# Sparse attention of a two-layer trunk: float32 operands replaced by two float16 parts in three passes

## The chip, the cores and the metric

One core of one Trainium2 chip runs the whole program. The metric is the time of one execution on the device in microseconds (us). An engine takes its instructions in an order that is fixed when the kernel is built.

## What is computed

A trunk of two layers over 512 tokens of width 1024. Each layer first normalises, projects and runs two branches (an RWKV-7 recurrence and a sparse attention), merges them with gates and projects again; then comes attention into 256 memory tokens, then a SwiGLU (layer 0) or eight experts (layer 1). The change lies in the sparse attention, cut here to its core (top_k is 128, eight heads of 64, one shared key and value head):

```python
logits = einsum('bqhd,bsd->bqhs', qib, k_idx32) * (IDX_DIM ** -0.5)
score = einsum('bqhs,bqh->bqs', relu(logits), wb) * (IDX_HEADS ** -0.5)
score = where(admissible[None], score, NEG_INF)
_, sel = lax.top_k(score, top_k)
ks, vs = gather(k, sel), gather(v, sel)
s = einsum('bqhd,bqkd->bqhk', qb, ks) * (DSA_HEAD_DIM ** -0.5)
p = softmax(where(valid[:, :, None, :], s, NEG_INF), axis=-1)
out = einsum('bqhk,bqkd->bqhd', p, vs)
```

## The kernel before

Matmuls with weights already run as float16 pairs: a float32 operand is kept as a high part and a low part (the remainder), and three passes (high by high, low by high, high by low) go into one PSUM bank. `split_ps` (L197) makes such a pair from a PSUM bank: ScalarE writes the high part, then VectorE subtracts it from the bank and writes the low part. The sparse attention does not do so: its operands are float32.

A layer is put together from generators that are stepped by a string (`ORDER`, L1633): `r` the recurrence, `d` keys and queries of the sparse attention, `s` its selection, `a` its attention, `g` the sixteen gate projections, `b` the branch projections. A scheduler then fixes each engine's order of instructions; the string only sets who comes first when several could go. Gates, recurrence and sparse attention therefore stand interleaved in the queue of TensorE (PE).

- `keys_queries` (L396) projects keys, values and index keys, normalises and rotates them, transposes them on PE, and copies them out of PSUM: `kT` (L421, ScalarE), `ikT` (L422, VectorE), `vt` (L409, ScalarE). `queries` (L459) does so for `iqT` and `qT`, by one ScalarE copy per bank (L487). Each key is stored twice, on partitions 0 to 63 and 64 to 127, and a pair of heads shares one tile: head e of a pair lies on row half e.
- `select` (L489), for the blocks b = 1 to 3 of 128 queries with n = 128(b+1) keys: for each of eight heads one float32 matmul of 64 rows by n columns into a bank of the two-bank group `att` (L503), a relu on ScalarE (L505), a weighted sum on VectorE (L507, L509); then sixteen rounds of MAX8 and MATCH_REPLACE on VectorE (L513, L514), which leave a mask.
- `attend` (L517), for each block, each half jp of the heads and each row half e: two score matmuls (L529) into `att` banks; VectorE adds the mask and takes the maximum (L530); ScalarE takes the exponential and scales by the reciprocal sum (L534, L538). After a `yield`, which lets the next attend's scores come first: transposes of the probabilities into `att` banks (L546), one copy of each bank to float32 `pT` (L547, on ScalarE for the first two key tiles and on VectorE for the others), and the product with the values (L553), whose output takes 64 partitions, half e of the bank `po`. After e = 1 the bank is split into `ybh` and `ybl` and stored.

The changed functions, with their callers:

Of the kernel before, what the change touches and what calls it, by code (L numbers as in the profile page):

```python
# [54 lines left out]
class Kern:  # L55
# [315 lines left out]
    def dsa(self, l, hh, hl, ybd, cx):  # L371
# [13 lines left out]
        qT = dp.tile([P, 4, SEQ], F32, name="qT")  # L385
        masks = [dp.tile([P, (b + 1) * P], BF, name=f"mask{b}") for b in range(NT)]
        ip = pool("dsai", 1, c1)
        iqT = ip.tile([P, 4, SEQ], F32, name="iqT")
        ikT = ip.tile([P, SEQ], F32, name="ikT")
# [3 lines left out]
        def keys_queries():  # L393
            with ExitStack() as c2:
# [5 lines left out]
                for i in range(2):  # L400
# [8 lines left out]
                    nc.scalar.activation(vt[:, t2, :], p[:, :, 64:128], AF.Copy, scale=1 / SW)  # L409
# [11 lines left out]
                    nc.scalar.copy(kT[:, cs].rearrange("p (t c) -> p t c", t=2), pv[:, :, 0, :])  # L421
                    nc.vector.tensor_copy(ikT[:, cs].rearrange("p (t c) -> p t c", t=2), pv[:, :, 1, :])  # L422
# [17 lines left out]
        def attends():  # L440
            todo = []
            for b in range(NT):
                if b == 0:
                    c2 = ExitStack()
                    dw = pool("dsav", 1, c2)
                if b == 2:
                    next(todo.pop(0), None)
                    c2.close()
                    c1.close()
                    dw = pool("dsaw", 2, cx)  # L450
                for jp in range(2):
                    for e in range(2):
                        todo.append(self.attend(dw, b, jp, e, masks[b], qT, kT, vt, qs, ybd))
                        next(todo[-1])
                        if len(todo) > 1:
                            next(todo.pop(0), None)
                yield
            next(todo.pop(0), None)
            cx.close()  # L459
        return keys_queries(), selects(), attends()  # L460

    def queries(self, pp, hh, hl, c, c0, dst, tabs, qs):
# [3 lines left out]
        for cc in range(2):  # L466
            ps = self.proj_tok2([c(c0 + 256 * cc, c0 + 256 * cc + 256)], hh, hl)
            for i in range(2):
# [15 lines left out]
                for j in range(4):  # L484
                    nc.tensor.transpose(pt[:, j * P:(j + 1) * P], qr[:, j // 2, 2 * (j % 2):2 * (j % 2) + 2, :].rearrange("p a b -> p (a b)"),
                                        self.ident)
                nc.scalar.copy(dst[:, 2 * cc:2 * cc + 2, 2 * i * P:(2 * i + 2) * P].rearrange("p j (t c) -> p t j c", t=2),  # L487
                               pt.rearrange("p (t j c) -> p t j c", t=2, j=2))

    def select(self, dw, b, m, iqT, ikT, iw):  # L490
# [9 lines left out]
        for h in range(8):  # L500
            hs = slice((h % 2) * 64, (h % 2) * 64 + 64)
            pl = self.bank("att", "pl")
            nc.tensor.matmul(pl[:, :n], lhsT=iqT[hs, h // 2, bs], rhs=ikT[hs, :n], start=True, stop=True)  # L503
# [13 lines left out]
    def attend(self, dw, b, jp, e, mask, qT, kT, vt, qs, ybd):  # L517

        nc = self.nc
        n = (b + 1) * P  # L520
        bs = slice(b * P, (b + 1) * P)
        es = slice(e * 64, e * 64 + 64)
        nm = 2 * P if b < 2 else SEQ
        s2 = dw.tile([P, 2, nm], F32, name="s2", bufs=2)
        mx, nb, sm, rv = (dw.tile([P, 2], F32, name=x, bufs=2) for x in ("mx", "nb", "sme", "rv"))
        q2 = qs[:, b, 4 * jp + e:4 * jp + e + 3:2]
        for i in range(2):
            pl = self.bank("att", "psc")
            nc.tensor.matmul(pl[:, :n], lhsT=qT[es, 2 * jp + i, bs], rhs=kT[es, :n], start=True, stop=True)  # L529
            nc.vector.tensor_tensor_reduce(s2[:, i, :n], pl[:, :n], mask, 1.0, -3.0e38, OP.add, OP.max, mx[:, i:i + 1])  # L530
        nc.vector.scalar_tensor_tensor(nb, mx, -1.0, q2, OP.mult, OP.mult)
        for i in range(2):
            h = 4 * jp + 2 * i + e
            nc.scalar.activation(s2[:, i, :n], s2[:, i, :n], AF.Exp, bias=nb[:, i:i + 1], scale=qs[:, b, h:h + 1],  # L534
                                 accum_out=sm[:, i:i + 1])
        nc.vector.reciprocal(rv, sm)
        for i in range(2):
            nc.scalar.activation(s2[:, i, :n], s2[:, i, :n], AF.Copy, scale=rv[:, i:i + 1])  # L538
        yield
        pT = dw.tile([P, nm // P, 2 * P], F32, name="pT", bufs=1)  # L540
        for k2 in range(0, b + 1, 2):
            m = min(2, b + 1 - k2)
            pp = self.bank("att", "pp")
            for x in range(2 * m):
                kt = k2 + x // 2
                nc.tensor.transpose(pp[:, x * P:(x + 1) * P], s2[:, x % 2, kt * P:(kt + 1) * P], self.ident)  # L546
            (nc.scalar.copy if k2 == 0 else nc.vector.tensor_copy)(  # L547
                pT[:, k2:k2 + m, :], pp[:, 0:2 * m * P].rearrange("p (k c) -> p k c", k=m))
        if e == 0:
            self.po = self.bank("po", "po")  # L550
        po = self.po
        for kt in range(b + 1):
            nc.tensor.matmul(po[es, 0:2 * P], lhsT=vt[:, kt, :], rhs=pT[:, kt, :], start=kt == 0, stop=kt == b)  # L553
        if e == 1:
            yh = dw.tile([P, 2, P], F16, name="ybh")
            yl = dw.tile([P, 2, P], F16, name="ybl")
            self.split_ps(yh, yl, po[:, 0:2 * P].rearrange("p (j t) -> p j t", j=2))
            for d, y in zip(ybd, (yh, yl)):
                nc.sync.dma_start(d[2 * jp:2 * jp + 2, :, bs].rearrange("j p t -> p j t"), y)
# [1195 lines left out]
```

## Time and profile before

| | |
|---|---|
| median of 3 runs | 2184.46 us (2177.66 to 2187.46) |
| the profiled execution | 2181.56 us, span 2179.8 us |
| PE busy | 2038.4 us (94%) |
| VectorE (DVE) busy | 1368.0 us (63%) |
| ScalarE (ACT) busy | 987.9 us (45%) |
| GpSimd (POOL) busy | 325.7 us (15%) |
| mean granted TensorE clock | 0.962 |

A busy time counts an engine's instructions from start to end; matmuls overlap in the pipeline, so the distance between starts, and not the duration, says what one costs. An idle time is put down to what ended it. The sparse attention runs between about 80 and 500 us (layer 0) and 1080 and 1500 us (layer 1). In a form such as 64*128 64x512 the first pair is the rows and columns of the array that the matmul uses. A float32 matmul has two records.

### The profile page before, as it was taken

The numbers are of one execution on the slowest core, as the hardware profiler recorded it, in microseconds if no ns is written. First come the engines' busy times: TensorE is split into PE (matmuls) and PEld (weight loads), VectorE is DVE, ScalarE is ACT, GpSimd is POOL, SyncE is SP. The second block draws the span as 40 slices with busy tenths as digits, with TensorE's granted clock in tenths as the row PEclk, the third lists the DMA queues.
The fourth block names the chain that finished last, engine by engine and source line by source line (L and its number), as shares of the span: only waits on it lengthen the run. The fifth ranks groups of instructions, "written<-read, shape, count | busy, mean of one in ns | idle before, by whom it ended". The sixth has DMA issues, their size and how long they took to land. (4 is left out here: it accounts for less than half of the span.)

```text
span 2179.8 us, 40496 instructions
## 1 busy us (share of the span) xinstructions
PE 2038.4 (94%) x16712; PEld 1317.0 (60%) x16712; DVE 1368.0 (63%) x2326; ACT 987.9 (45%) x1545; POOL 325.7 (15%) x338
## 2 busy tenths in 40 slices
PE   8998899898998999999999989999799799999997
PEld 4664455464464544444583555535355599999996
DVE  6767975644665433322567995463554688888886
ACT  5533334441353333321443443442233378887883
POOL 2351500002010000000251340001200120000002
PEclk9998999999998999999999999999899899999998
DMA  7342324342542333333334222334151799999993
GB/s 223 101 101 75 111 61 114 78 150 60 191 150 67 104 100 104 104 99 102 116 82 106 84 85 73 96 89 144 55 178 35 251 354 383 360 355 345 343 344 132
DMA packets 339538, 332.48 MB, mean 153 GB/s; under 512 B 93697, under 2 KB 255617, under 8 KB 339346
## 3 DMA queue, kind: packets, MB, share of 16 engines
q1 hardware_dynamic: 328240, 306.03, 44.2%
q10 hardware_dynamic: 8482, 15.39, 2.1%
q0 software_dynamic: 2624, 8.40, 1.1%
q8 instruction: 133, 2.18, 0.4%
q14 instruction: 59, 0.48, 0.1%
HBM read 297.05 MB, written 32.72 MB: 151 GB/s over the span
## 5 line engine op out<-in xcount | busy, mean ns | idle before, releaser
L263 ACT ACTIVATE whi<-raw 128x1024 f16<-128x1024 f32 (+3 forms) x242 | 226.9, 939 | 501.6 <-PE pf L285 278.0
L268 DVE SCALAR_TENSOR_TENSOR wlo<-raw,whi 128x1024 f16<-128x1024 f32 (+3 forms) x208 | 233.3, 1123 | 215.0 <-ACT whi L263 202.0
L1510 DVE SCALAR_TENSOR_TENSOR ewlo<-eraw,ewhi 128x1024 f16<-128x1024 f32 x265 | 320.2, 1219 | 57.7 <-ACT ewhi L1509 56.8
L285 PEld LDWEIGHTS <-whi 128*128 128x128 f16 x1888 | 183.6, 99 | 245.9 <-issue 48.0
L1509 ACT ACTIVATE ewhi<-eraw 128x1024 f16<-128x1024 f32 x265 | 276.6, 1053 | 77.7 <-PE py L1569 34.1
L1524 PE MATMUL pe<-XT,ewhi 128*128 128x144 f16 x2816 | 206.1, 226 | 0.5 <-issue 0.5
L1524 PEld LDWEIGHTS <-ewhi 128*128 128x128 f16 x2816 | 183.2, 98 | 1.2 <-issue 0.6
L285 PE MATMUL pf<-hh,whi 128*128 128x512 f16 x448 | 172.4, 385 | 5.0 <-ACT qe L481 2.6
L285 PE MATMUL pf<-hl,whi 128*128 128x512 f16 x448 | 172.0, 384 | 0.0
L285 PEld LDWEIGHTS <-wlo 128*128 128x128 f16 x944 | 92.0, 99 | 116.5 <-issue 15.9
L285 PE MATMUL pf<-fh,whi 128*128 128x512 f16 x336 | 127.3, 379 | 0.0
L285 PE MATMUL pf<-fl,whi 128*128 128x512 f16 x336 | 127.3, 379 | 0.0
L266 POOL TENSOR_TENSOR wlo<-raw,whi 128x1024 f16<-128x1024 f32 (+3 forms) x34 | 60.3, 1772 | 410.8 <-ACT raw L265 262.9
L1524 PE MATMUL pe<-XT,ewlo 128*128 128x144 f16 x1408 | 116.8, 226 | 0.1
L285 PE MATMUL pf<-hh,wlo 128*128 128x512 f16 x448 | 112.7, 385 | 0.0
L1569 PE MATMUL py<-HT,ewhi 128*128 128x144 f16 x1408 | 103.9, 227 | 0.1
L164 POOL TENSOR_TENSOR rs<-rs,nrm_e 128x1 f32<-128x1 f32 x28 | 16.7, 596 | 520.1 <-DVE rs L163 520.1
L1524 PEld LDWEIGHTS <-ewlo 128*128 128x128 f16 x1408 | 94.1, 98 | 0.3 <-DVE ewlo L1510 0.3
L1569 PEld LDWEIGHTS <-ewhi 128*128 128x128 f16 x1408 | 92.5, 98 | 0.3 <-issue 0.2
L285 PE MATMUL pf<-fh,wlo 128*128 128x512 f16 x336 | 79.4, 379 | 0.0
L345 PE MATMUL ptok<-whi,hh 128*128 128x256 f16 (+1 forms) x320 | 75.8, 276 | 0.0
L345 PE MATMUL ptok<-whi,hl 128*128 128x256 f16 (+1 forms) x320 | 75.5, 276 | 0.0
(437 smaller groups left out, 3886.0 us busy)
## 6 DMA issues: line engine op xcount, KB each, us to landing
raw<-in_w_in_dram SPq DMA_DIRECT2D x76, 512.0 KB
eraw<-in_moe_wg_dram SPq DMA_DIRECT2D x16, 2048.0 KB
eraw<-in_moe_wu_dram SPq DMA_DIRECT2D x16, 2048.0 KB
eraw<-in_moe_wd_dram SPq DMA_DIRECT2D x16, 2048.0 KB
eraw<-in_moe_wg_dram SPq DMA_DIRECT2D x8, 1536.0 KB
eraw<-in_moe_wu_dram SPq DMA_DIRECT2D x8, 1536.0 KB
eraw<-in_moe_wd_dram SPq DMA_DIRECT2D x8, 1536.0 KB
raw<-in_ffn_wg_dram SPq DMA_DIRECT2D x22, 512.0 KB
```

Source lines behind the costliest of these rows:

```text
L164: nc.gpsimd.tensor_tensor(out, out, self.nrm_e[:, :n], OP.pow)
L263: nc.scalar.activation(hi, raw, AF.Copy, scale=SW)
L266: nc.gpsimd.tensor_tensor(lo, raw, hi, OP.subtract)
L268: nc.vector.scalar_tensor_tensor(lo, raw, SW, hi, OP.mult, OP.subtract)
L285: self.nc.tensor.matmul(p, lhsT=w[:, k, :], rhs=x[k], start=first, stop=last)
L345: mm(p, lhsT=x[:, k0 + k, ts], rhs=w[:, k, :], start=k0 == 0 and t % 2 == 0 and first, stop=k0 + kg == kt and last, skip_group_check=True)
L1509: nc.scalar.activation(r[0], w, AF.Copy, scale=SW)
L1510: nc.vector.scalar_tensor_tensor(r[1], w, SW, r[0], OP.mult, OP.subtract)
L1524: mm(p[:, i * n:(i + 1) * n], lhsT=w[:, k, :], rhs=XT[:, k, h, :], start=z == 0, stop=z == len(ms) - 1)
L1569: mm(ps[d], lhsT=w[:, i, d * P:(d + 1) * P], rhs=HT[:, k, h, :], start=k == 0 and w is wh and h == 0 and d % per == 0, stop=k == FT - 1 an ...
```

## The change

Queries, keys, values, index queries, index keys and probabilities are kept as two float16 tiles each (suffix h and l), made by `split_ps`. A new function `scores` issues three passes for both heads of a pair, alternating between the row halves, into two banks, for `select` and for `attend`. `attend` now takes four heads (both row halves) at once, so that there is one call where there were two; the product with the values alternates between the two column halves of `po`. The probabilities are scaled by 64 before they are split, and the output by 1/(64*64).

```diff
-        kT = dp.tile([P, SEQ], F32, name="kT")
-        vt = dp.tile([P, NT, 64], F32, name="vt")
+        two = lambda p, n, *s: [p.tile([P, *s], F16, name=n + x) for x in "hl"]
+        kT = two(dp, "kT", SEQ)
+        vt = two(dp, "vt", NT, 64)
...
-                    nc.scalar.activation(vt[:, t2, :], p[:, :, 64:128], AF.Copy, scale=1 / SW)
+                    self.split_ps(vt[0][:, t2, :], vt[1][:, t2, :], p[:, :, 64:128])
...
-                    nc.scalar.copy(kT[:, cs].rearrange("p (t c) -> p t c", t=2), pv[:, :, 0, :])
-                    nc.vector.tensor_copy(ikT[:, cs].rearrange("p (t c) -> p t c", t=2), pv[:, :, 1, :])
+                    for g, dst in enumerate((kT, ikT)):
+                        self.split_ps(*[d[:, cs].rearrange("p (t c) -> p t c", t=2) for d in dst], pv[:, :, g, :])
...
-                    for e in range(2):
-                        todo.append(self.attend(dw, b, jp, e, masks[b], qT, kT, vt, qs, ybd))
-                        next(todo[-1])
-                        if len(todo) > 1:
-                            next(todo.pop(0), None)
+                    todo.append(self.attend(dw, b, jp, masks[b], qT, kT, vt, qs, ybd))
+                    next(todo[-1])
+                    if len(todo) > 1:
+                        next(todo.pop(0), None)
...
-                nc.scalar.copy(dst[:, 2 * cc:2 * cc + 2, 2 * i * P:(2 * i + 2) * P].rearrange("p j (t c) -> p t j c", t=2),
-                               pt.rearrange("p (t j c) -> p t j c", t=2, j=2))
+                self.split_ps(*[d[:, 2 * cc:2 * cc + 2, 2 * i * P:(2 * i + 2) * P].rearrange("p j (t c) -> p t j c", t=2) for d in dst],
+                              pt.rearrange("p (t j c) -> p t j c", t=2, j=2))
...
+    def scores(self, qT, j, bs, kT, n):
+
+        pls = [self.bank("att", "psc") for _ in range(2)]
+        for i, (x, y) in enumerate(((0, 0), (1, 0), (0, 1))):
+            for e in range(2):
+                es = slice(e * 64, e * 64 + 64)
+                self.nc.tensor.matmul(pls[e][:, :n], lhsT=qT[x][es, j, bs], rhs=kT[y][es, :n], start=i == 0, stop=i == 2)
+        return pls
...
-            (nc.scalar.copy if k2 == 0 else nc.vector.tensor_copy)(
-                pT[:, k2:k2 + m, :], pp[:, 0:2 * m * P].rearrange("p (k c) -> p k c", k=m))
...
+                self.split_ps(*[t[:, k2:k2 + m, :] for t in pT[e]], pp[:, 0:2 * m * P].rearrange("p (k c) -> p k c", k=m), self.SP)
...
         for kt in range(b + 1):
-            nc.tensor.matmul(po[es, 0:2 * P], lhsT=vt[:, kt, :], rhs=pT[:, kt, :], start=kt == 0, stop=kt == b)
+            for i, (x, y) in enumerate(((0, 0), (1, 0), (0, 1))):
+                for e in range(2):
+                    nc.tensor.matmul(po[e * 64:e * 64 + 64, 0:2 * P], lhsT=vt[x][:, kt, :], rhs=pT[e][y][:, kt, :],
+                                     start=kt == 0 and i == 0, stop=kt == b and i == 2)
```

What the scheduler makes of it, at three places. First PE in layer 0 at the scores of block 3, first pair of heads. A number behind `psc` is a bank, one for each head. Before:

```order
L553 MATMUL po_3683<-pT_3672,vt_523 64x256 x2
L529 MATMUL psc_3692<-kT_522,qT_525 128x512
L553 MATMUL po_3683<-pT_3672,vt_523 64x256
L529 MATMUL psc_3695<-kT_522,qT_525 128x512
L285 LDWEIGHTS whi_4898
```

And in the changed kernel:

```order
L523 MATMUL psc_3800<-kTh_522,qTh_527 128x512
L523 LDWEIGHTS qTl_528
L523 MATMUL psc_3800<-kTh_522,qTl_528 128x512
L523 LDWEIGHTS qTh_527
L523 MATMUL psc_3800<-kTl_523,qTh_527 128x512
L560 LDWEIGHTS vth_524
L560 MATMUL po_3770<-pT1l_3745,vth_524 64x256
L523 LDWEIGHTS qTh_527
L523 MATMUL psc_3801<-kTh_522,qTh_527 128x512
L523 LDWEIGHTS qTl_528
L523 MATMUL psc_3801<-kTh_522,qTl_528 128x512
```

The three passes of one head (bank 3800) now stand before the three of the other (3801), with a product of the previous attend between them, and do not alternate as the source has them.

Second PE in layer 0 at the scores of block 0 (n = 128), in the changed kernel, where one head's bank is 3377 and the other's 3378:

```order
L523 MATMUL psc_3377<-kTh_522,qTh_527 128x128
L523 LDWEIGHTS qTh_527
L523 MATMUL psc_3378<-kTh_522,qTh_527 128x128
L523 LDWEIGHTS qTl_528
L523 MATMUL psc_3377<-kTh_522,qTl_528 128x128
L523 LDWEIGHTS qTl_528
L523 MATMUL psc_3378<-kTh_522,qTl_528 128x128
L523 LDWEIGHTS qTh_527
L523 MATMUL psc_3377<-kTl_523,qTh_527 128x128
L523 LDWEIGHTS qTh_527
L523 MATMUL psc_3378<-kTl_523,qTh_527 128x128
```

Here the two heads alternate, as the source has it.

Third DVE in layer 0 at the probabilities of block 2, between the steps of the recurrence's inverse (`pr`, `z`, `x`; lines 999 and 1001 before, 1010 and 1012 after). Before:

```order
L536 RECIPROCAL rv<-sme 128x2
L547 COPY pT<-pp 128x256
L1001 TENSOR_REDUCE x_3892<-pr 128x64
L268 SCALAR_TENSOR_TENSOR wlo<-raw,whi 128x256
L999 TENSOR_TENSOR pr<-z_3891,t2f 128x1024
```

And in the changed kernel:

```order
L542 RECIPROCAL rv<-sme 128x4
L1010 TENSOR_TENSOR pr<-z_4038,t2f 128x1024
L1070 SCALAR_TENSOR_TENSOR mf<-gt,pf 128x512
L204 SCALAR_TENSOR_TENSOR pT0l<-pp,pT0h 128x512
L204 SCALAR_TENSOR_TENSOR pT0l<-pp,pT0h 128x256
L1070 SCALAR_TENSOR_TENSOR mf<-gt,pf 128x512
L1012 TENSOR_REDUCE x_4039<-pr 128x64
L268 SCALAR_TENSOR_TENSOR wlo<-raw,whi 128x256
L204 SCALAR_TENSOR_TENSOR pT1l<-pp,pT1h 128x512
L204 SCALAR_TENSOR_TENSOR pT1l<-pp,pT1h 128x256
```

Where DVE copied one bank in two of an attend, it now has a low part to write for each of them, behind the same long steps.

## Rows read from the trace of the kernel before

**Rows 1.** Windows: us; busy and count by engine; granted clock; DMA share; GB/s

```profile
200.00:290.00 90.00, 80.29 (x691) 48.53 (x689) 84.64 (x180) 36.86 (x63) 39.27 (x38) 0.94 0.25 80
290.00:400.00 110.00, 110.00 (x719) 62.76 (x719) 62.60 (x170) 49.45 (x108) 9.99 (x7) 1.00 0.32 89
400.00:440.00 40.00, 34.29 (x135) 14.29 (x134) 26.15 (x53) 14.44 (x33) 2.02 (x3) 0.91 0.40 93
440.00:520.00 80.00, 79.30 (x774) 48.66 (x775) 32.45 (x72) 24.87 (x50) 13.39 (x10) 0.98 0.39 120
...
1200.00:1290.00 90.00, 77.44 (x658) 47.43 (x656) 83.69 (x166) 38.65 (x66) 46.61 (x44) 0.94 0.32 98
1290.00:1440.00 150.00, 149.56 (x974) 82.74 (x970) 81.44 (x228) 62.49 (x138) 8.60 (x7) 0.98 0.29 76
1440.00:1460.00 20.00, 15.24 (x47) 6.08 (x45) 16.84 (x27) 6.47 (x15) 0.15 (x1) 0.74 0.29 82
```

**Rows 2.** Timeline of PE from 1461 us: start, us, engine, line, operation, tiles, form

```profile
1461.42 1.12 PE L529 MATMUL psc<-kT,qT 64*128 64x512 f32 x2
1462.47 0.39 PE L285 MATMUL pf<-yah,whi 128*128 128x512 f16 x1
1462.70 0.38 PE L285 MATMUL pf<-yal,whi 128*128 128x512 f16 x1
1462.91 0.38 PE L285 MATMUL pf<-yah,whi 128*128 128x512 f16 x1
```

**Rows 3.** Timeline of PE at 63.8 us: two float32 matmuls on different row halves

```profile
63.87 0.69 PE L715 MATMUL pz<-x,wa 64*128 64x512 f32 x1
63.88 0.69 PE L729 MATMUL pa<-x,wa 64*128 64x512 f32 x1
...
64.93 0.39 PE L285 MATMUL pf<-hh,whi 128*128 128x512 f16 x1
```

**Rows 4.** Timeline of PE at 1299 us: float32 products on alternating column halves

```profile
1299.17 0.45 PE L885 MATMUL pS<-UV,AM 128*64 128x64 f32 x8
1299.56 0.71 PE L529 MATMUL psc<-kT,qT 64*128 64x128 f32 x4
```

**Rows 5.** Matmuls of lines 503, 529, 553: ns min/median/max, first and last start, forms

```profile
L503 PE MATMUL pl<-ikT,iqT x96: 376/587/1006, 142.1 to 1290.6; 64*128 64x256 f32 x32, 64*128 64x384 f32 x32, 64*128 64x512 f32 x32
...
L529 PE MATMUL psc<-kT,qT x128: 272/482/1219, 284.3 to 1474.9; 64*128 64x128 f32 x32, 64*128 64x256 f32 x32, 64*128 64x384 f32 x32, 64*128 64x512 f32 x32
...
L553 PE MATMUL po<-pT,vt x160: 379/379/688, 306.9 to 1492.9; 128*64 128x256 f32 x160
```

**Rows 6.** Evictions, subtractions and small operations, the same columns

```profile
L547 ACT COPY pT<-pp x32: 372/575/603, 300.7 to 1486.4; 128x512 f32<-128x512 f32 x24, 128x256 f32<-128x256 f32 x8
L547 DVE COPY pT<-pp x16: 402/548/693, 395.5 to 1489.8; 128x256 f32<-128x256 f32 x8, 128x512 f32<-128x512 f32 x8
...
L201 DVE TENSOR_TENSOR hl<-pT,hh x16: 673/682/693, 29.9 to 1068.3; 128x512 f16<-128x512 f32 x16
...
L531 DVE SCALAR_TENSOR_TENSOR nb<-mx,qs x32: 142/153/161, 287.9 to 1476.5; 128x2 f32<-128x2 f32 x32
```

**Rows 7.** Waits of PE, 1290:1500, then 280:520 us: total, times, longest

```profile
PE psc L529 <- DVE pT L547: 4.7, 2, 4.2
...
PE pp L546 <- DVE mx L530: 3.3, 3, 1.9
PE po L553 <- ACT pT L547: 2.3, 1, 2.3
```

**Rows 8.** Timeline of PE from 1443 us: a wait, and the passes behind it

```profile
1448.12 2.07 PE L529 MATMUL psc<-kT,qT 64*128 64x512 f32 x2 [4.22 <-DVE pT L547]
...
1454.88 0.61 PE L285 MATMUL pf<-yah,whi 128*128 128x512 f16 x1
1455.28 0.63 PE L285 MATMUL pf<-yal,whi 128*128 128x512 f16 x1
...
1458.26 0.39 PE L285 MATMUL pf<-yah,whi 128*128 128x512 f16 x1
```

More of the change, by code (lines that the diff above doesn't have):

```diff
@@ L500, in select @@
         for h in range(8):
-            hs = slice((h % 2) * 64, (h % 2) * 64 + 64)
-            pl = self.bank("att", "pl")
-            nc.tensor.matmul(pl[:, :n], lhsT=iqT[hs, h // 2, bs], rhs=ikT[hs, :n], start=True, stop=True)
+            if h % 2 == 0:
+                pls = self.scores(iqT, h // 2, bs, ikT, n)
+            pl = pls[h % 2]
             r = dw.tile([P, SEQ], F32, name="relu", bufs=2)
@@ L531, in attend @@
[L531 to L535, printed above, removed]
+            for e, pl in enumerate(self.scores(qT, 2 * jp + i, bs, kT, n)):
+                h = 2 * i + e
+                nc.vector.tensor_tensor_reduce(s4[:, h, :n], pl[:, :n], mask, 1.0, -3.0e38, OP.add, OP.max, mx[:, h:h + 1])
@@ L536, in attend @@
+        nc.vector.scalar_tensor_tensor(nb, mx, -1.0, qs[:, b, 4 * jp:4 * jp + 4], OP.mult, OP.mult)
+        for h in range(4):
+            nc.scalar.activation(s4[:, h, :n], s4[:, h, :n], AF.Exp, bias=nb[:, h:h + 1], scale=qs[:, b, 4 * jp + h:4 * jp + h + 1],
+                                 accum_out=sm[:, h:h + 1])
         nc.vector.reciprocal(rv, sm)
-        for i in range(2):
-            nc.scalar.activation(s2[:, i, :n], s2[:, i, :n], AF.Copy, scale=rv[:, i:i + 1])
+        for h in range(4):
+            nc.scalar.activation(s4[:, h, :n], s4[:, h, :n], AF.Copy, scale=rv[:, h:h + 1])
@@ L539, in attend @@
         yield
[L540 to L546, printed above, removed]
-            (nc.scalar.copy if k2 == 0 else nc.vector.tensor_copy)(
-                pT[:, k2:k2 + m, :], pp[:, 0:2 * m * P].rearrange("p (k c) -> p k c", k=m))
@@ L549, in attend @@
-        if e == 0:
-            self.po = self.bank("po", "po")
-        po = self.po
-        for kt in range(b + 1):
-            nc.tensor.matmul(po[es, 0:2 * P], lhsT=vt[:, kt, :], rhs=pT[:, kt, :], start=kt == 0, stop=kt == b)
[L554 to L559, printed above, removed]
+        pT = [[dw.tile([P, nm // P, 2 * P], F16, name=f"pT{e}{x}", bufs=1) for x in "hl"] for e in range(2)]
@@ new lines, in attend @@
+        for e in range(2):
+            for k2 in range(0, b + 1, 2):
+                m = min(2, b + 1 - k2)
+                pp = self.bank("att", "pp")
+                for x in range(2 * m):
+                    kt = k2 + x // 2
+                    nc.tensor.transpose(pp[:, x * P:(x + 1) * P], s4[:, 2 * (x % 2) + e, kt * P:(kt + 1) * P], self.ident)
+                self.split_ps(*[t[:, k2:k2 + m, :] for t in pT[e]], pp[:, 0:2 * m * P].rearrange("p (k c) -> p k c", k=m), self.SP)
+        po = self.bank("po", "po")
@@ L562, in rwkv @@
+        self.split_ps(yh, yl, po[:, 0:2 * P].rearrange("p (j t) -> p j t", j=2), 1 / (SW * self.SP))
+        for d, y in zip(ybd, (yh, yl)):
+            nc.sync.dma_start(d[2 * jp:2 * jp + 2, :, bs].rearrange("j p t -> p j t"), y)
+    SP = 64.0
     def rwkv(self, l, cx, sx, hh, hl, ya):
```

22 lines of the change are left out of this document (11 added, 11 removed).

## The prediction

> **What bounds the kernel now.** I first read the windows of the stretches in which the sparse attention runs [rows 1]. From 290 to 400, 440 to 520 and 1290 to 1440 us PE is busy all but 1.2 of 340 us, at a granted clock of 0.98 to 1.00, while DVE is busy 0.4 to 0.6 of the time and ACT less: there PE's work is the time. From 200 to 290 and 1200 to 1290 us, where the selections run, it is the other way round: DVE is busy 84.6 and 83.7 of 90 us and PE has 10 to 13 us to spare. And for 60 us (400 to 440, 1440 to 1460) PE waits for others: 34.3 of 40 and 15.2 of 20 us busy, the clock at 0.91 and 0.74.
>
> Then the prices, from the timeline of PE [rows 2]. A float16 pass of 512 columns takes 0.21 us from start to start (1462.70 to 1462.91); that is the 2.4 GHz level, 0.42 ns a column. The scores of one head against 512 keys in float32 take 1.05 us (1461.42 to 1462.47). Four passes of 512 columns would be 0.86 us, so float32 costs **four passes**, and the 0.19 us left over is what it takes to go into the 64-row form of the array and out of it. The two float32 matmuls on different row halves confirm it: both together take 1.06 us (63.87 to 64.93), as long as one alone [rows 3]. **Two row halves run at the same time.** So do two column halves: eight records of 64 columns, alternating, are over after 0.39 us with the way in [rows 4]; each record is two passes, 0.054 us, and one after another they alone would be 0.43.
>
> **The change part by part.** PE first. Lines 503, 529 and 553 hold 48 heads (two records each) at 256, 384 or 512 columns, 64 heads at 128 to 512, and 80 products of 256 columns [rows 5]. In columns that is 18,432 for the selections, 20,480 for the scores of attend and 20,480 for the products: 59,392 in all. At four passes and 0.42 ns they cost 31.0, 34.4 and 34.4, together 99.8 us of streaming.
>
> Three passes one after another would be 23.2, 25.8 and 25.8, together 74.8 us. With every pair of halves side by side it would be half of that, 37.4. Which of the two it is, the order tells, not the source: of the 56 pairs of heads only 19 alternate throughout (7 of 8 at n = 128, 9 of 16 at 256, 3 of 16 at 384, none of 16 at 512). The others stand as three passes of one head and then three of the other, mostly with other work between. PE takes matmuls in order, so the second head can't start beside the first. Counting pass by pass what stands next to a pass of the other half, the selections save 2.8 of their 23.2 us, the scores of attend 7.3 of 25.8, and the products, which mostly alternate, 11.4 of 25.8. That leaves 20.4, 18.5 and 14.4, together 53.3 us: **46.5 us less streaming**, 10.6 in the selections and 35.9 in attend.
>
> The way into and out of a form is paid per block of such matmuls. By the order there are 86 blocks of scores and 39 of products before, 83 and 40 after: nothing changes. The transposes are the same 160. At n = 128 a pass is 0.054 us and a weight load may not hide behind it; with 48 such passes this is at most a few us, and I take nothing.
>
> What counts of it: in attend 380 of the 440 us from 290 to 520 and 1290 to 1500 are not of the waiting kind [rows 1], so I take 6/7 of 35.9, 30.8 us. Of the selections those of block 1 (4,096 columns, before 6.9, after 3.1 us) run before 200 and 1200 us, where PE has work queued: 3.8 us. The other 6.8 us fall where DVE is the bound: nothing.
>
> DVE and ACT next. Each of the 48 banks of probabilities was copied once, 32 by ACT and 16 by DVE; now ACT writes 48 high parts and DVE 48 low parts. A low part from 512 columns costs 0.68 us, and from 256 the copy's 0.41 is the nearest row [rows 6]. DVE: 32 at 0.68 and 16 at 0.41 are 28.3, less the old 16 copies, 8.8; the low parts of queries and index queries, 16 at 0.68, 10.9; those of keys and values, 8 at up to 0.41, 3.3; 16 fewer of the small scale steps at 0.153, 2.5 less. Together 31.2 us more. ACT: 16 more copies at up to 0.60 and four of keys, 11 us at most; it is busy under half the time, so nothing. Of DVE's sum the probabilities lie in stretches where it is busy 0.4 to 0.6 of the time, and are covered by PE; the index queries and keys come before 200 and 1200 us and I count nothing for them either. The eight low parts of the queries, 5.4 us, come while DVE is the bound: counted in full, between 0 (PE has waiting work of its own) and 5.4.
>
> Waits: a bank of probabilities is now held until the subtraction is done. PE waited for copies of these banks in three of the 48 cases, 7.0 us, and 3.3 us for the maxima, which also hold `att` banks [rows 7]. The cost of the longer hold lies between 0 (other work stands between in the order) and 48 subtractions fully exposed, 28.3 us; I take 0, as 45 of 48 were covered. If the cover is gone, see the last rival.
>
> The sum: 30.8 + 3.8 - 5.4 = 29.2 us less. The profiled execution took 2181.56 us, so 2152.4; the median of the runs is 2.9 us above it, so **2155 us**. A difference of 0.5%, about 11 us, is what a measurement of this kernel can tell from none.
>
> One rule speaks against the products. Our rows 4 show loads and passes of the two column halves at one pace, with nothing between pairs. The Trainium skill (TensorE: Matmul & The Clock Gate, Part 3, "What overlaps and what doesn't") says that a weight load overlaps matmuls in flight only when the row group differs, and the two column halves use the same rows. By that rule the products would gain nothing from alternating, which is the third rival below; rows 4 speak against it, though only for float32 passes of 64 columns.
>
> **The rivals.**
> - *PE bounds all of it.* With PE lighter, gates and projections move up into the selections, and the 60 waiting us shrink too: all 46.5 us count, and 2184.5 - 46.5 is **2138 us**. For it: gate projections are free to move. Against: 84 of 90 us of DVE.
> - *The halves do not overlap in float16*, so the change doesn't do what it says: 74.8 us of streaming are left, attend goes from 68.8 to 51.6, and 6/7 of 17.2 is 14.7; block 1 of the selections gives 1.7, the low parts take 5.4: 11.0 us less, **2173 us**. Against it stand rows 3; for it, that they show float32 only.
> - *The column halves alone do not overlap*: the 11.4 us of the products are lost, 9.8 of them on the path: **2165 us**. The rule of the Trainium skill named above (TensorE: Matmul & The Clock Gate, Part 3) would give this.
> - *Two more long waits.* Once, PE waited 4.22 us for a copy of probabilities that stood behind long steps on DVE; the clock then fell to half, and the passes up to 1458.26 took 0.40 in place of 0.21 us [rows 8], 10.1 us for the work of 5.1. Such a wait costs 4.2 + 5.0 = 9.2 us. One copy in 16 on DVE did that; with 48 low parts on DVE it would be three, two more: **2174 us**.
> - *Slower: those waits become the rule.* The order puts the low parts of block 2 behind the long inverse steps, for both halves. If five more of them make PE wait so, the price is 46 us, and 2155 + 46 is **2201 us**. The point from which the result is slower by over 0.5% (2195) is 40/9.2, so the fifth such wait. For it: PE will reach these waits sooner, as it has less to do before. Against: from 290 to 400 us DVE is busy only 62.6 of 110.
>
> **How the numbers follow.** The forecast 0.43 (by itself 2145 to 2166: the low parts of the queries at nothing, or another wait or so); PE bounds all 0.18; no overlap 0.12; column halves alone 0.07; two more waits 0.12; slower 0.08. A time under 2173.5 us is faster by over 0.5%: the forecast less 0.03, the first and the third rival, and about half of the two that end at 2173 and 2174, 0.76 in all, which I call 0.75. Slower is 0.08, with 0.01 for what I have not seen; the rest, 0.16, is within 0.5%. The range from 2132 to 2182 leaves out the slower case and the ends of the others: fast, if PE's lighter queue also shortens the recurrence's steps; slow, if one wait comes on top of no overlap.
>
> **What would show it.** In the profile after, an alternating pair at n = 128 or 256 should start both heads within 0.01 us and take three passes' time, and a head at 512 should take 0.65 us plus 0.2 alone. A pair of products, one for each column half, should take 0.11 us. PE's busy time from 290 to 520 and 1290 to 1500 should be down, the stretches before 290 and 1290 as long as now. DVE should have about 30 us more in all. Rows of the waits on low parts (`pT0l`, `pT1l`) of over 4 us, with a granted clock under 0.9 behind them, would show the slow rivals; passes of two halves one after another would show the overlap wrong. If the gain is there but selections, not attend, are shorter, my placing of it is wrong.

## The result, and the profile after

The changed kernel takes **2162.88 us** (median of 7 runs, 2148.25 to 2169.51), against 2181.26 us of the kernel before in the same comparison: ratio 0.9896, 95% interval 0.9855 to 0.9936. It is 18 us faster. The time was predicted as 2155 (2132 to 2182), so the sign and the range hold. The price of the passes holds too; the way from there to the time does not, as the experiments show.

The profiled execution took 2148.25 us, the shortest of the seven; its span is 2146.4 us at a mean granted clock of 0.952. The median of the seven clocks is 0.941. The busy times of its page:

```profile
PE 2001.3 (93%) x16904; PEld 1309.3 (61%) x16904; DVE 1395.6 (65%) x2350; ACT 992.3 (46%) x1565; POOL 320.4 (15%) x338
```

DVE gained 27.6 us (31.2 predicted), ACT 4.4. PE lost 37.1 us of busy time. The windows of the stretches of [rows 1], in the changed kernel (same columns):

```profile
200.00:290.00 90.00, 81.14 (x736) 49.22 (x736) 81.01 (x175) 36.58 (x60) 37.12 (x38) 0.96 0.30 89
290.00:400.00 110.00, 108.10 (x766) 60.00 (x765) 71.28 (x194) 50.71 (x116) 10.21 (x7) 0.98 0.37 95
400.00:440.00 40.00, 30.01 (x194) 14.92 (x196) 30.36 (x53) 19.47 (x45) 1.73 (x3) 0.74 0.52 128
440.00:520.00 80.00, 78.52 (x728) 52.42 (x727) 34.89 (x74) 22.70 (x44) 14.23 (x11) 0.83 0.30 92
1200.00:1290.00 90.00, 77.58 (x753) 49.19 (x755) 83.89 (x173) 37.68 (x64) 41.41 (x38) 0.96 0.30 93
1290.00:1440.00 150.00, 139.22 (x914) 75.47 (x911) 93.95 (x229) 61.37 (x143) 9.39 (x8) 0.91 0.35 93
1440.00:1460.00 20.00, 18.18 (x151) 10.27 (x149) 10.21 (x23) 12.98 (x30) 1.55 (x2) 0.59 0.42 96
```

From 200 to 290 and from 1200 to 1290 us the engines are about as busy as before, as predicted. Where PE was said to be the time, from 440 to 520 us and from 1290 to 1440 us, it is still busy for 78.5 of 80 and 139.2 of 150 us, but the granted clock fell from 0.98 to 0.83 and 0.91. Part of the time that the passes gave up came back as a slower clock.

**The passes themselves do what was predicted.** The timeline of PE at the scores of block 1 (256 keys): first a pair whose heads alternate, then one where the order has them one after the other.

```profile
349.21 0.28 PE L523 MATMUL psc<-kTh,qTh 64*128 64x256 f16 x2
349.33 0.27 PE L523 MATMUL psc<-kTh,qTl 64*128 64x256 f16 x2
349.44 0.27 PE L523 MATMUL psc<-kTl,qTh 64*128 64x256 f16 x2
...
352.29 0.28 PE L523 MATMUL psc<-kTh,qTh 64*128 64x256 f16 x1
352.34 0.28 PE L812 MATMUL pB<-ct,bkb 64*128 64x64 f32 x2
352.41 0.27 PE L523 MATMUL psc<-kTh,qTl 64*128 64x256 f16 x1
352.46 0.22 PE L812 MATMUL pB<-ct,bkb 64*128 64x64 f32 x1
352.52 0.27 PE L523 MATMUL psc<-kTl,qTh 64*128 64x256 f16 x1
352.53 0.27 PE L523 MATMUL psc<-kTh,qTh 64*128 64x256 f16 x1
352.64 0.27 PE L523 MATMUL psc<-kTh,qTl 64*128 64x256 f16 x1
352.75 0.27 PE L523 MATMUL psc<-kTl,qTh 64*128 64x256 f16 x1
```

Two records per row ("x2") start together and the next two 0.11 us later; one after the other, each record alone takes those 0.11 us, except where the heads meet (352.52 and 352.53). The products on the two column halves do the same, a pair every 0.11 us with their weight loads hidden:

```profile
470.16 0.27 PE L560 MATMUL po<-pT1h,vth 128*64 128x256 f16 x1
470.19 0.27 PE L560 MATMUL po<-pT0l,vth 128*64 128x256 f16 x1
470.27 0.27 PE L560 MATMUL po<-pT1h,vtl 128*64 128x256 f16 x1
470.30 0.27 PE L560 MATMUL po<-pT0h,vth 128*64 128x256 f16 x1
```

To compare kernels I add up PE's matmuls by kind: for each the distance to the next start, at most its own duration, halved where the granted clock is 0.5. This "work" is what they would take at the full clock. Before and after, in the profiled executions: products 39.7 and 19.7 us, scores of attend 43.7 and 23.6, selections 32.9 and 24.3; all of PE 1973.5 and 1915.8. Of the 57.7 us between them 9 lie in lines that the change does not touch, so a few us of work are not read as a difference here.

**So PE's work fell by 57.7 us, and the time by 18.** The other side is the clock: span times (1 minus the mean clock) is what a run gives up at half clock, idle time at half clock included. It is 81 us in the runs of before (median clock 0.963, the runs beside e1) and 127 in those of the changed kernel (0.941). The work is that of the profiled execution, the one that gave up least: its span is 33.4 us shorter than that of before, with 57.7 us less work, 20.8 us more lost by matmuls at half clock (65.0 before, 85.8 after) and 3.5 us more of all else.

All kernels that follow, each beside runs of the kernel before on the same chip (its median was between 2180 and 2184 us there). The clock is the median of the runs; the work is from the profiled execution.

| kernel | median us | ratio to before (95%) | clock | given up to the clock, us | PE work, us |
|---|---|---|---|---|---|
| before | 2180 to 2184 | 1 | 0.961 to 0.963 | 81 to 85 | 1973.5 |
| changed | 2162.88 | 0.9896 (0.9855 to 0.9936) | 0.941 | 127 | 1915.8 |
| e1 one head after the other | 2154.45 | 0.9865 (0.9837 to 0.9892) | 0.951 | 106 | 1925.2 |
| e2 alternation fixed | 2142.73 | 0.9820 (0.9790 to 0.9849) | 0.950 | 107 | 1907.1 |
| e3 float32, four heads | 2145.75 | 0.9839 (0.9810 to 0.9868) | 0.956 | 95 | 1937.2 |
| e12 float32, half by half | 2172.24 | 0.9964 (0.9938 to 0.9990) | 0.961 | 85 | 1962.2 |
| e6b low parts of probabilities zero | 2145.71 | 0.9833 (0.9810 to 0.9856) | 0.950 | 107 | 1911.9 |
| e9 float16 scores only, fixed | 2139.29 | 0.9812 (0.9785 to 0.9839) | 0.955 | 96 | 1914.7 |
| e10 float16 products only, fixed | 2148.03 | 0.9847 (0.9826 to 0.9869) | 0.954 | 99 | 1930.5 |
| e16 as e9, copies on ScalarE | 2138.51 | 0.9793 (0.9766 to 0.9820) | 0.955 | 96 | 1910.4 |
| e15 changed, 27 us of work added | 2152.66 | 0.9849 (0.9822 to 0.9876) | 0.957 | 93 | 1943.4 |
| e7 fillers in the second chain | 2262.63 | 1.0389 (1.0362 to 1.0415) | 0.921 | 179 | 1918.4 |
| e13 fillers late | 2183.02 | 1.0003 (0.9981 to 1.0025) | 0.939 | 133 | 1911.1 |

The changed kernel is the slow one of its family. Four kernels that differ from it in little (e1, e2, e6b, e15) are 8 to 20 us faster, whether they take work away or add it, at a clock of 0.950 to 0.957; of its own seven runs two take 2148 and 2150 us at 0.952 and 0.950, and five 2160 to 2170 us at 0.939 to 0.944. A gain against this kernel alone is therefore not yet the worth of what an experiment took out.

### The profile page after: what moved, and what is told of

The parts are those of the page before. It is cut to its first block, busy times and chain, and to the rows that moved or that the text cites. A ratio compares the mean times of both kernels' runs of the same rounds, so it can differ in the third digit from the quotient of the medians.

```text
span 2146.4 us, 40963 instructions
## 1 busy us (share of the span) xinstructions
PE 2001.3 (93%) x16904; PEld 1309.3 (61%) x16904; DVE 1395.6 (65%) x2350; ACT 992.3 (46%) x1565; POOL 320.4 (15%) x338
## 4 chain that ended last, share of the span: by engine, by line
PE 32%; DVE 8%; DMA 4%; ACT 2%; issue 2%; POOL 1%; SPq 1%; DVEq 0%; ACTq 0%; POOLq 0%
PE pe L1535 11%; PE py L1580 6%; PE pf L285 4%; PE ptok L327 2%; DVE iacc L514 1%; DVE m L513 1%; DVE wlo L268 1%; DMA eraw<-in_moe_wu_dram 1%; PE py L911 1%; PE pyt L1556 1%; PE psc L523 1%; PE pS L902 1%; PE pS L896 1%; PE pf L297 1%; PE py L917 1%
## 5 line engine op out<-in xcount | busy, mean ns | idle before, releaser
L1520 ACT ACTIVATE ewhi<-eraw 128x1024 f16<-128x1024 f32 x265 | 277.4, 1054 | 79.8 <-PE py L1580 33.4
```

Source lines behind the costliest of these rows:

```text
L1520: nc.scalar.activation(r[0], w, AF.Copy, scale=SW)
```

## The experiments

**e1: no alternation.** In `scores` and in the products, head (or column half) outermost, and the order fixed:

```diff
-        for i, (x, y) in enumerate(((0, 0), (1, 0), (0, 1))):
-            for e in range(2):
...
+        for e in range(2):
+            for i, (x, y) in enumerate(((0, 0), (1, 0), (0, 1))):
```

> The changed kernel with the six passes of a pair issued one head after the other, and the products one column half after the other. By the built order the three lines then stream 69.2 us against 53.7 in the changed kernel and 99.8 before. Theory A (streaming saved on PE is time where PE bounds, about 0.74 of it): 15.5 us more streaming, 11 us slower than the changed kernel, 2174 us. Rival B (what counts is something else in the change, the alternation is worth nothing because PE gets its time back elsewhere): 2163 us, no difference from the changed kernel. In the trace the starts of the second head should lie behind the third pass of the first.

The edit undoes the running side by side in the products only: counted in the traces, 54 of their 240 passes start within 0.04 us of another, against 194 in the changed kernel. Of the 336 passes of the scores and selections 160 still do (178 in the changed kernel), although in the order the second head's three passes stand behind the three of the first. PE in layer 0 at a selection of e1:

```profile
181.16 0.29 PE L524 MATMUL psc<-ikTh,iqTh 64*128 64x256 f16 x2
181.28 0.28 PE L524 MATMUL psc<-ikTh,iqTl 64*128 64x256 f16 x2
181.39 0.28 PE L524 MATMUL psc<-ikTl,iqTh 64*128 64x256 f16 x2
```

So the second head's starts do not lie behind the third pass of the first, as was expected, and PE's work rises by 9.4 us in place of 15.5: in the products (28.3 for 19.7), not in the scores. The kernel is not 11 us slower than the changed one, it is no slower at all (2154.45), and gives up 106 us to the clock in place of 127. Against the changed kernel theory A falls. Against e2 below, which fixes the order too and ran beside e1, it about holds: 18.1 us more work and 11.7 us more time, though the two intervals overlap a little.

**e2: alternation fixed.** Each pass of a pair is ordered behind the one before, so that the heads alternate at 384 and 512 keys too:

```diff
+                if m is not None:
+                    self.order(k.ins, m.ins)
+                m = k
```

> The changed kernel with the order of a pair's six passes fixed, so that the two heads alternate at 384 and 512 columns too. By the built order the streaming is 43.4 us against 53.7. Theory A: 10.3 us less streaming, of which 0.74 count, 7.6 us faster than the changed kernel, 2155 us. Rival B (the freed time is given back, by waits for two banks at once or by a lower clock): 2163 us or more, with longer waits on the score banks or more time at half the granted clock.

20 us faster than the changed kernel, more than the 7.6 expected. Of these, 8.7 are PE's work (selections 19.5, scores 21.4, products 19.1); the rest is clock, 107 us in place of 127.

**e3 and e12: the gain without float16.** e3 keeps the new grouping (pairs, four heads in one attend) and puts every operand back to float32. e12 also undoes the alternation: the two heads of one half first, then the two of the other, and likewise the products, in a fixed order. The cut shows what both have in common.

```diff
-                self.nc.tensor.matmul(pls[e][:, :n], lhsT=qT[x][es, j, bs], rhs=kT[y][es, :n], start=i == 0, stop=i == 2)
...
+            self.nc.tensor.matmul(pls[e][:, :n], lhsT=qT[es, j, bs], rhs=kT[es, :n], start=True, stop=True)
```

> The changed kernel with everything in float32 as before, but with its pairs and its four heads in one attend. The two heads' float32 matmuls then stand next to each other and overlap: by the built order 71.7 us of streaming (before 99.8, changed 53.7), and no low parts on VectorE. Theory A: 28.1 us less streaming than before, 0.74 of it is 21 us, 2160 us, so about the whole gain without any float16. Rival B (only the float16 passes bring the gain, the new grouping nothing): 2181 us, as before. Rival C (the new grouping costs by holding banks longer): over 2185 us.

> All in float32, four heads in one attend, but the two heads of one row half first and then the two of the other, and the products of one column half and then of the other, as before the change: the grouping without the alternation. By the profiles of before and of the float32 kernel with alternation this gives back 13.6 us of products and 9.3 of scores on PE (at full clock). Theory (the gain of the float32 kernel with four heads comes from the halves running side by side): 12 to 23 us slower than that kernel's 2145.8, 2158 to 2169 us. Rival (it comes from the grouping, which gives PE more to choose from between two steps of an attend): 2146 us, as with alternation.

Float32 with alternation takes 2145.75 us, 14 less than theory A expected: **the whole gain and more, with no float16 pass and no low part.** Its products take 26.1 us of work and its scores 34.4, in place of 39.7 and 43.7, because the float32 matmuls of the two halves, now neighbours in the order, run side by side as those of [rows 3] did. The timelines of PE at the scores of two heads with 256 keys (four records), first e3, then e12, where both heads lie on the same half:

```profile
342.45 0.70 PE L522 MATMUL psc<-kT,qT 64*128 64x256 f32 x4
```

```profile
343.83 1.13 PE L537 MATMUL psc<-kT,qT 64*128 64x256 f32 x4
```

Two heads in 0.70 us, against 1.13. Without alternation (35.3 and 41.6) the kernel is at 2172.24: alternation alone is worth 0.0125 of the time, 27 us, for 25.0 us of work (12 to 23 us were expected), and the grouping about 8, by its interval 2 to 14. Here work and time agree.

**e9 and e10: float16 for one part alone**, the alternation fixed as in e2. e9 keeps float16 for queries and keys, e10 for probabilities and values; the other part is as in e3.

> Float16 pairs for the scores and selections alone, with the alternation fixed; probabilities, values and their products in float32, so no low parts of probabilities on VectorE. PE's work by the profiles so far: products 26.1, scores 21.4, selections 19.5, together 67 us at full clock, against 60 with all in float16 and 92.5 with all in float32 (four heads each). Theory now (PE's work in the recurrence's stretch is worth little, VectorE's low parts cost there): as fast as all in float16 or faster, 2133 to 2143 us. Rival (only PE's work counts): 7 us slower than all in float16, 2150 us.

> Float16 pairs for the probabilities and values alone; queries, keys, index queries and index keys in float32, four heads in one attend. PE's work: products 19.1, scores 34.4, selections 32.0, together 85.5 us against 92.5 with all in float32. Theory now (the low parts of the probabilities on VectorE cost more than the 7 us of PE are worth): slower than all in float32 by 4 to 10 us, 2150 to 2156 us. Rival (only PE's work counts): 2139 us.

With e2 and e3 this makes four: float16 nowhere 0.9839, products 0.9847, scores 0.9812, both 0.9820. The scores bring about 0.0027 (6 us) in either row, the products cost 0.0008; both lie inside the intervals. e9 agrees with the theory, e10 only in that there is no gain. 7 us less work in the products bought nothing.

**e6 and e6b: the low parts of the probabilities.** e6 left VectorE's subtractions out and let the third pass read the high part again. e6b replaces that by a tile of zeros.

```diff
-                self.split_ps(*[t[:, k2:k2 + m, :] for t in pT[e]], pp[:, 0:2 * m * P].rearrange("p (k c) -> p k c", k=m), self.SP)
+                nc.scalar.activation(pT[e][:, k2:k2 + m, :], pp[:, 0:2 * m * P].rearrange("p (k c) -> p k c", k=m), AF.Copy,
+                                     scale=self.SP)
```

> The changed kernel without the low parts of the probabilities: VectorE's 48 subtractions are left out, and the third pass of each product uses the high part, so that PE does the same work (the output lacks the probabilities' low parts). Theory A (the subtractions lie beside other work): within 4 us of the changed kernel, 2159 to 2165 us. Rival B (the longer hold of the banks and VectorE's extra 28 us give back what PE saved): 10 to 20 us faster than the changed kernel, 2143 to 2153 us.

> The changed kernel without the 48 subtractions that make the low parts of the probabilities: the third pass of each product reads a tile of zeros, so PE does the same passes (the low parts of the probabilities are left out of the output). Theory now: between the end of the first recurrence chain and the start of the second the recurrence's own path sets the time (145.6 us in layer 0 before, 144.6 after, though PE's work there fell by 18 us at full clock), and the subtractions lengthen it, since the inverse's steps on VectorE stretch over 42 us in place of 37 in each layer: 10 us faster than the changed kernel, 2153 us. Rival, as predicted first (the subtractions are covered): 2160 to 2165 us, no difference.

e6 answers nothing: the values it changes decide how many tokens each expert receives, and behind 2200 us its trace holds the path for overfull experts (10,208 matmuls of `pe<-oXT,ewhi`); it took 4517.55 us. e6b is 17 us faster than the changed kernel for the same passes on PE (the intervals of the ratios just touch), and faster than both sides expected. That the subtractions cost this much is not shown: e2 keeps all 48 and takes 2142.73, and between e9 and e2 (order fixed, the products once in float32 without subtractions and once in float16 with them) lie 0.0008 of the time, 2 us. PE's work differs by 3.9 us, and 20 us less are given up to the clock. The way I had thought of, by a stretched inverse, is not borne out: from the first to the last of the inverse's products (`pr`) the changed kernel takes 42.4 and 42.7 us, e6b 40.1 and 38.3, but e9, without any subtraction, 43.0 and 41.0, and e15, with all of them, 38.0 and 37.2.

**e15: work added.** Sixteen dense passes before the products of each attend of blocks 2 and 3:

```diff
         po = self.bank("po", "po")
+        for _ in range(16 if b > 1 else 0):
+            nc.tensor.matmul(po, lhsT=self.hh_[:, 0, 0:P], rhs=self.hh_[:, 0, :], start=True, stop=True)
```

> The changed kernel with sixteen dense float16 passes of 128x512 before the products of each attend of blocks 2 and 3, into the attend's own bank, which the products then overwrite: 128 passes at 0.21 us, 27 us more work for PE at full clock, nearly all between the end of the first recurrence chain and the end of the second. Theory (after the change that stretch is not set by PE's work but by the recurrence's own steps and by the clock): the time stays within 8 us of the changed kernel's 2162.9, 2155 to 2171 us, with more PE time at full clock in the stretch and less half clock. Rival (PE's work is the time there, as predicted first): 27 us slower, 2190 us.

27.6 us more work on PE, and the time is 2152.66: not 27 us slower, but 10 us faster, 2 more than the theory allowed; the intervals of the two ratios overlap, so that it is faster is not shown. The windows from the end of the first recurrence chain to the start of the second, and from there to its end, in both layers. The changed kernel:

```profile
319.80:464.50 144.70, 131.71 (x1116) 75.41 (x1115) 94.56 (x214) 73.98 (x164) 8.17 (x8) 0.89 0.40 100
464.50:493.20 28.70, 28.31 (x230) 21.09 (x231) 7.39 (x20) 2.21 (x4) 1.64 (x1) 0.78 0.40 134
1341.70:1472.40 130.70, 118.92 (x1042) 67.04 (x1042) 81.88 (x180) 67.13 (x149) 7.16 (x8) 0.91 0.39 100
1472.40:1499.90 27.50, 27.50 (x254) 20.86 (x252) 8.48 (x22) 3.78 (x7) 1.64 (x1) 0.90 0.32 102
```

With the work added:

```profile
324.20:464.90 140.70, 133.39 (x1152) 73.70 (x1151) 92.51 (x211) 72.38 (x162) 8.17 (x8) 0.96 0.40 102
464.90:495.50 30.60, 30.60 (x258) 22.29 (x256) 8.27 (x21) 3.47 (x7) 1.64 (x1) 0.86 0.34 113
1339.90:1470.20 130.30, 122.25 (x1117) 69.34 (x1117) 79.45 (x177) 65.79 (x144) 8.13 (x8) 0.96 0.39 102
1470.20:1503.80 33.60, 33.22 (x246) 23.10 (x246) 8.36 (x21) 2.73 (x5) 1.64 (x1) 0.80 0.36 122
```

Before the change these stretches were:

```profile
331.50:477.00 145.50, 139.79 (x1066) 76.27 (x1063) 80.91 (x189) 69.77 (x149) 8.91 (x8) 0.98 0.38 99
477.00:516.70 39.70, 39.00 (x271) 22.94 (x272) 12.19 (x27) 5.34 (x9) 12.37 (x9) 0.96 0.46 149
1353.00:1495.90 142.90, 137.46 (x1046) 74.38 (x1046) 77.02 (x181) 67.19 (x141) 7.00 (x8) 0.96 0.38 98
1495.90:1547.70 51.80, 47.05 (x296) 26.07 (x295) 14.22 (x29) 6.08 (x11) 13.89 (x10) 0.90 0.38 122
```

Layer 0's stretch ahead of the second chain is 145.5 us long before, 144.7 after and 140.7 with the added passes. The length does not follow PE's work in it (136.4, 118.4 and 129.0 us at full clock). In its place the granted clock moves: 0.98, 0.89, 0.96. Layer 1's follows it in part: 142.9, 130.7 and 130.3 us, for 132.3, 107.5 and 119.2 us of work; there the change bought 12.2 us, and the added passes cost nothing.

**e7 and e13: dense passes inside the second chain.** e7 is e2 with four dense passes after each of seven steps of the chain; e13 is e9 with them after the last four steps only, in another bank.

```diff
+                for _ in range(4):
+                    f = mm(dm, lhsT=self.hh_[:, 0, 0:P], rhs=self.hh_[:, 0, :], start=True, stop=True)
+                    self.order(f.ins, last)
+                    last = f.ins
```

> The kernel with the fixed alternation, and in the second recurrence chain of each layer four dense float16 passes of 128x512 after each of seven steps, written to a bank that nobody reads: 56 passes, 12 us more work. There the profile showed PE busy with 64-column matmuls at half clock (17 us of half clock in layer 0 from 484 us, 24 us in layer 1 from 1481 us). Theory (the clock falls because PE has too little dense work, and this is what takes the gain back): the half clock in the two chains goes nearly away, 12 us of loss less for 12 us of work, 2139 to 2147 us against 2142.7. Rival (the clock falls for another reason): half clock as before in these stretches, 2155 us.

> The kernel with float16 scores, float32 products and fixed alternation (2139.3 us, the fastest so far) with four dense float16 passes of 128x512 after each of the last four steps of the second chain of each layer, into the bank of the attend that is free by then, so that no gate projection is moved (the first try held a bank of the gates and moved them): 32 passes, 6.7 us more work. In that kernel the second chain of layer 0 shows 8.4 us lost to half clock, that of layer 1 none. Theory (the clock falls for want of dense work): the loss in layer 0's second chain goes under 3 us, and the time comes to 2136 to 2142 us. Rival (the clock is not moved by them): the loss stays, 2146 us.

Both miss. e7's bank belonged to the gate projections and was held from early on, so that these moved behind the chain; windows as above, first to second chain and second chain:

```profile
314.50:428.10 113.60, 82.96 (x851) 54.86 (x848) 79.34 (x196) 54.83 (x128) 2.41 (x4) 0.67 0.20 41
428.10:463.00 34.90, 34.90 (x270) 22.09 (x268) 6.66 (x18) 2.67 (x4) 1.64 (x1) 1.00 0.13 42
```

Where the gates were taken out the clock fell to 0.67; in the chain, with dense passes from its first step on, it stayed at 1.00 (where e2 gave up 5.6 us of 28.1). The moved gates are a second difference between the two, so that the passes did this is not shown. Taking the gates out also shortened the stretch to 113.6 us with only 59.3 us of work in it, 31 us less than in the changed kernel: what sets its length is then neither PE's work alone nor a fixed path of the recurrence. In e13 the late passes did not bring the clock back. It had fallen before the first of them, and they ran at half clock themselves, four in 1.89 us:

```profile
465.30:500.40 35.10, 35.10 (x213) 22.97 (x211) 6.24 (x17) 0.63 (x1) 1.64 (x1) 0.60 0.00 1
...
476.16 0.47 PE L907 MATMUL pS<-UV,AM 128*64 128x64 f32 x2
...
476.97 1.89 PE L919 MATMUL dm<-hh 128*128 128x512 f16 x4
```

The first row is a window, the others are of the timeline of PE. For 6.7 us of passes e13 is 44 us slower than e9 and gives up 37 us more to the clock; part of it, because in layer 1 the branch projections (20.9 us) that stood inside e9's second chain now stand behind it.

**e16: copies on ScalarE.** e9 with all 48 copies of the probabilities on ScalarE.

```diff
-                (nc.scalar.copy if k2 == 0 else nc.vector.tensor_copy)(
+                nc.scalar.copy(
```

> Float16 scores, float32 products, fixed alternation (2139.3 us), with all 48 copies of the probabilities on ScalarE; VectorE loses its 16, 8.8 us of the rows of before. Theory (VectorE's work between the inverse's steps costs time, as the 28 us of subtractions cost 17): about 5 us faster, 2134 us. Rival (only the holding of the score banks until the subtraction costs, not VectorE's time): no difference, 2139 us.

2138.51 us; the ratio is 0.0019 under that of e9 and inside its interval, so the question stays open. e9 and e16 beat both the kernel before and the changed one.

## Why the prediction was right, and where it was wrong

That the time lies in the range is in part luck. PE's work fell by 57.7 us, where the sum counted 34.6 (30.8 and 3.8); 46 us more were given up to the clock, which is not in the sum. The two errors pull in opposite directions.

**The terms of PE held.** Streaming was to fall by 46.5 us: 20.0 in the products, 15.9 in the scores, 10.6 in the selections. Measured as work it fell by 20.0, 20.1 and 8.6, together 48.7. That not every pair would run side by side was needed for that: e2, where more do, has 7.0 us less in scores and selections. The reason given was wrong, though: that PE takes matmuls in order, "so the second head can't start beside the first". In e1 it does, from three places behind. By the order 9 of 16 pairs at 256 columns and 3 of 16 at 384 were to alternate, 54 and 18 of 96 passes; in the changed kernel's trace 84 and 50 run side by side. At 512 columns, where other work or a wait stands between the heads, none of 96 does, and 68 in e2. The rival without overlap in float16 is refuted by the starts above. The rival in which PE bounds all (2138) gave the right size of the saving and the wrong time for it. Refuted too is the one by which column halves alone don't overlap, by a pair of products every 0.11 us. The Trainium skill (TensorE: Matmul & The Clock Gate, Part 3, "What overlaps and what doesn't") says that a weight load overlaps matmuls in flight only where the row group differs. The trace does not agree: with a load before each pass, those pairs still start every 0.11 us. Two slips of the prediction change nothing: rows 4 show passes but no loads, and the chances of a time under 2173.5 us add up to 0.77, not 0.76.

**The step that failed is what counts of it**: "in attend 380 of the 440 us ... are not of the waiting kind, so I take 6/7". That PE is busy 110 of 110 us says that it could do no more there; it does not say that the stretch gets shorter when work is taken away. By the table the first 36 us of work that are taken away (before to e3, 1973.5 to 1937.2) give 34 us, nearly all. Below that the times no longer line up with the work: at 1907 to 1916 us there are times from 2138 to 2163 without added passes, and at 1943.4 (e15) 2152.66. The prediction counted the whole saving at one rate, and the changed kernel lies 21 us of work beyond e3.

**Left out of the sum: the clock.** The prediction priced it only behind a wait, 9.2 us each, as a rival. Measured it is the largest term after the passes: 46 us more given up than before (127 less 81), against 61 us less of span times clock (medians 2099.6 and 2038.8). Some of it does follow a wait, as that rival said. In layer 0 the maximum of a score bank stood on VectorE behind a step of the inverse, which waited 7.54 us for a transfer; PE waited 6.14 us for it, then ran at half clock. Rows of VectorE, then of PE:

```profile
401.88 1.88 DVE L1010 TENSOR_TENSOR pr<-t1h,a 128x1024 f32<-128x1024 f32 x1 [7.54 <-DMA scrN<-ttn]
403.68 0.55 DVE L537 CUSTOM_DVE_ANT_0 s<-psc,mask 128x384 f32<-128x384 f32 x1
...
404.29 1.54 PE L554 MATMUL pp<-ct,s 128*128 128x128 f32 x6 [6.14 <-DVE mx L537]
405.63 0.63 PE L285 MATMUL pf<-yah,whi 128*128 128x512 f16 x1
```

That was a wait for a maximum, not for a low part, and the next longest in the stretches of the attention is 3.3 us; so neither the rival of two more long waits nor the slower one is what happened. Other half-clock time has no such wait before it. From 480.5 to 497.5 us it lies inside the second chain of layer 0, where PE is busy with passes of 64 columns:

```profile
479.29 0.33 PE L896 MATMUL pS<-UV,AM 128*64 128x64 f32 x2
479.55 0.32 PE L902 MATMUL pS<-TT,art 64*64 64x64 f32 x2
480.25 0.33 PE L896 MATMUL pS<-UV,AM 128*64 128x64 f32 x2 [0.39 <-DVE TT L904]
...
484.14 0.47 PE L911 MATMUL py<-UV,AM 128*64 128x64 f32 x2
484.55 0.47 PE L917 MATMUL py<-TT,art 64*64 64x64 f32 x2
```

A pair takes 0.26 us at first and 0.40 us later; the one idle time of PE in this chain, 0.39 us, stands right before the fall. Before the change 16.2 us of dense projections stood between the steps of this chain, and 21.2 us in layer 1; in the changed kernel none, since PE reached them earlier or they stand behind. The chains give up 5.9 us at half clock before and 9.2 after; the stretches ahead of them 8.5 and 24.8.

**VectorE.** 31.2 us more were predicted, 27.6 measured. Whether the low parts of the probabilities are "covered by PE" is not settled: without them the changed kernel is 17 us faster (e6b), but with the order fixed they and their float16 products cost 2 us more than float32 products without them (e9 to e2). The bound of that term was 28.3, the value taken 0. The low parts of the queries were priced at 5.4 us and can't be told from nothing here: from the start to the first chain, and from layer 1's first `hh` tile to its first chain, it is 283.0 and 245.9 us before, 274.7 and 255.2 after, 1.0 us more in all.

**Not seen at all**: that float32 itself would gain from alternation. Rows 3 and 4 showed both overlaps for float32, and the prediction used them for the price of float16 only. Three passes for four are worth little here; neighbours on different halves are worth 27 us.

What stays open: why the changed kernel gives up 20 us more to the clock than e1, e2 and e6b, which differ little from it in PE's work. No trace shows it: the profiled execution of the changed kernel gave up 103 us, less than those of the three (114, 109 and 116).

## What to carry to other kernels

Before operands are split to save passes, put matmuls of different halves next to each other: in float32 that alone gave 27 us of the 34. To learn whether a busy engine is the bound, add work to it and look at the time; the busy share did not tell here. Compare an experiment with more than one kernel: against the changed one alone, taking passes' neighbours apart (e1), taking subtractions out (e6b) and putting work in (e15) all looked like gains. When PE gets lighter, compare span times clock and span times (1 minus clock) apart, since a saving on PE can return as a lower clock.

## What the runs showed of the hardware that was not expected

- The spread between runs of one kernel is for the most part the clock. The spans of the kernel before went from 2171.2 us at a clock of 0.967 to 2192.3 at 0.957; span times clock is 2099.6 and 2098.0 there, and 2091 to 2102 over all eleven runs beside e1.
- The granted clock fell to half in a stretch of passes of 64 columns in which PE was idle for 0.4 us only (0.26, then 0.40 us a pair). With dense passes between the steps from the first one on it was 1.00 (e7, where other work had moved too); four at a time, late, ran at half clock themselves (e13: 0.60 in that chain, 0.56 in layer 1's).
- Added matmuls made a kernel no slower: with 27.6 us of them the clock was 0.957 in place of 0.941 (e15). Part of that is no effect of theirs, as e1, e2 and e6b, without them, have 0.950 or 0.951.
- In e1 PE did not hold the passes of one row half back behind those of the other: the second head's first pass starts with the first head's first, though two more passes of the first stand ahead of it (181.16 us; 160 of the 336 passes start within 0.04 us of another).
